# Half of the ktile pairs of the second MLP products with 7 block products in place of 8

## The chip, the cores and the metric

One core of a Trainium2 chip runs the whole program. The metric is the device time of one execution in microseconds; three runs of the kernel before gave 2282.13 to 2282.56 us, median 2282.18 us.

## The reference, cut to what matters

Two decoder layers work on x of 256 tokens by 2048 features in float32. Each layer has an attention part and an MLP, and each of the four sub-layers adds its normalised output to the stream:

```python
def sq_relu_mlp(h, w1, w2):
    return jnp.square(jax.nn.relu(h @ w1)) @ w2
...
h = h + rms_norm(sq_relu_mlp(rms_norm(h, g_pre), w1, w2), g_post)
```

w1 is 2048 x 8192 and w2 is 8192 x 2048. The change concerns the second product of each MLP, hidden (256 x 8192) times w2.

## The kernel before, in words

Every large product is made of two-part operands: `split` (lines 238 to 246) writes a float32 operand as a high part in float32r (ScalarE, line 242, or 245 where a gain is multiplied in) and the rest as a low part (VectorE, line 243 or 246). A product of x and w is then three matmuls: high·high, high·low, low·high. The weights come as raw tiles of two ktiles (a ktile is 128 rows) by 1024 columns, 1 MB, by SyncE's queue (line 310, three buffers). `weights` splits each ktile into one `whi` and one `wlo` tile of 128 x 1024, five buffers of each (`NW`). So ScalarE and VectorE prepare weights while TensorE multiplies, and five ktiles are the farthest that they can be ahead.

`mlp` (line 620) goes over four blocks b of 2048 hidden features. In each, `ff1` computes hidden = relu(u·w1)², two calls of `job_T` of 1024 features (lines 405 and 409 are its matmuls of 512 and of 256 columns). The evacuation of a PSUM bank there is a ScalarE copy of 256 columns (L398), a VectorE addition (L399), and for every two banks relu and square on ScalarE (L628, L629) and a split into the tile `hT` (L242, L243). Then two calls of `job` (line 324, its matmul is line 361) multiply the 16 ktiles of the block by w2, for columns 0 to 1023 and 1024 to 2047: per ktile 2 token tiles x 2 column chunks x 3 = 12 matmuls of 128 x 512. The four sums of a `job` are evacuated into the tiles `m`, which stay in SBUF over all blocks: a ScalarE copy in block 0 (L670), a VectorE addition later (L672). After the last block `PostNorm` squares, scales (GpSimd, L589) and adds to the stream h.

The large SBUF tiles (8 KB a partition) share one pool, `A`, of 11 buffers (`NA`): in the MLP 4 for the input `uT`, 4 for `hT`, 2 for `m`, 1 for the gain. The stream h has a place of its own. The six scratch tiles `s2` serve the evacuations. PSUM has 8 banks: 4 `mm`, 2 `sb`, 2 `tb`. Small pieces of other work are queued in `bt` and let in between products by a credit of time (`tick`).

The order of each engine's instructions is fixed at build time by the scheduler of the kernel's framework, which takes instructions as they become ready and, among ready ones, the earliest in the program. An engine runs its own list strictly in that order.

## Time and profile before

| | |
|---|---|
| median of three runs | 2282.18 us |
| the profiled execution, its own time | 2280.53 us |
| its span in the trace | 2278.6 us |
| TensorE (PE) matmuls | 11949, busy 99% of the span |
| VectorE (DVE) busy | 1346.2 us, 59% |
| ScalarE (ACT) busy | 1250.0 us, 55% |
| GpSimd (POOL) busy | 51.9 us, 2%; it issues no DMA |
| DMA | 418.58 MB, 184 GB/s over the span |
| granted TensorE clock | 0.998 of full speed, 2.4 GHz |

The profiled execution's own time holds 1.9 us that lie outside its span. A busy matmul time is not time on the path: matmuls overlap in the array, so the distance between starts counts. Idle time of an engine that isn't the bottleneck costs nothing by itself.

### The profile page before, as it was taken

How to read it: one execution, taken by the hardware profiler on the slowest of the kernel's cores; microseconds unless marked ns; L12 is line 12 of the kernel's file. 1: busy time of each engine (PE TensorE's matmuls, PEld its weight loads, DVE VectorE, ACT ScalarE, POOL GpSimd, SP SyncE). 2: the span in 40 equal slices, each digit the busy share in tenths (PEclk: the TensorE clock that was granted, in tenths of full speed). 3: DMA queues.
4: the chain of work that ended last, by engine and by line, in shares of the span. 5: the costliest groups of instructions: out<-in, count | busy, mean ns of one | idle time of the engine just before them, and what ended most of it. 6: DMA issues, size and time to landing. Idle time of an engine off the chain costs nothing.

```text
span 2278.6 us, 30208 instructions
## 1 busy us (share of the span) xinstructions
PE 2255.6 (99%) x11949; PEld 1937.5 (85%) x11949; DVE 1346.2 (59%) x2059; ACT 1250.0 (55%) x1940; POOL 51.9 (2%) x44
## 2 busy tenths in 40 slices
PE   9999999999999999999999999999999999999997
PEld 9889887888888888887888888887888888888886
DVE  5877547544654554566565677847554554554555
ACT  5766547544644544555556666657554554554553
POOL 0000010000000000011000000001000000000002
PEclk9999999999999999999999999999999999999999
DMA  7844455565465555554554554555565555555553
GB/s 249 247 148 139 140 174 166 198 208 186 168 220 185 185 203 185 185 198 160 188 193 149 184 174 159 178 174 163 192 212 188 188 198 189 186 198 190 185 202 112
DMA packets 131177, 418.58 MB, mean 184 GB/s; under 512 B 6870, under 2 KB 7644, under 8 KB 130524
## 3 DMA queue, kind: packets, MB, share of 16 engines
q1 hardware_dynamic: 131036, 416.66, 54.3%
q8 instruction: 93, 1.52, 0.3%
q14 instruction: 48, 0.39, 0.1%
HBM read 414.54 MB, written 2.10 MB: 183 GB/s over the span
## 4 chain that ended last, share of the span: by engine, by line
PE 90%; issue 5%; DVE 2%; POOL 1%; ACT 1%; DMA 0%; DVEq 0%; POOLq 0%; SPq 0%; ACTq 0%
PE mm L361 27%; PE mm L405 19%; PE mm L409 10%; PE sb L361 6%; PE tb L361 6%; PE tb L405 4%; PE sb L405 4%; PE sb L409 2%; PE tb L409 2%; PE mm L435 2%; PE sb L539 2%; PE mm L443 2%; PE tb L283 1%; DVE h L603 1%; POOL m L589 1%
## 5 line engine op out<-in xcount | busy, mean ns | idle before, releaser
L246 DVE SCALAR_TENSOR_TENSOR wlo<-raw,gT,whi 128x512 fp32r<-128x512 f32 (+4 forms) x621 | 606.6, 1010 | 433.5 <-PE tb L409 208.2
L245 ACT ACTIVATE whi<-raw,gT 128x512 fp32r<-128x512 f32 (+4 forms) x621 | 551.2, 928 | 452.3 <-PE tb L405 238.0
L243 DVE TENSOR_TENSOR wlo<-raw,whi 128x1024 fp32r<-128x1024 f32 x304 | 376.6, 1245 | 356.8 <-ACT whi L242 356.8
L242 ACT ACTIVATE whi<-raw 128x1024 fp32r<-128x1024 f32 x304 | 320.7, 1061 | 384.5 <-PE mm L361 212.3
L405 PE MATMUL mm<-uT,whi 128*128 128x512 f32 x1952 | 503.5, 394 | 0.3 <-ACT z L845 0.3
L405 PEld LDWEIGHTS mm<-uT,whi 128*128 128x128 f32 x1952 | 346.9, 189 | 58.4 <-DVE s L399 0.7
L409 PEld LDWEIGHTS mm<-uT,wlo 128*128 128x128 f32 x1952 | 271.2, 190 | 22.3
L409 PE MATMUL mm<-uT,wlo 128*128 128x256 f32 x1952 | 280.3, 283 | 0.0
L361 PE MATMUL mm<-whi,hT 128*128 128x512 f32 x1024 | 280.3, 389 | 0.0
L361 PEld LDWEIGHTS mm<-whi,hT 128*128 128x128 f32 x1024 | 192.3, 188 | 39.7
L361 PE MATMUL mm<-whi,uT 128*128 128x512 f32 (+1 forms) x640 | 197.0, 398 | 0.0
L361 PE MATMUL mm<-wlo,hT 128*128 128x512 f32 x512 | 162.9, 389 | 0.0
L361 PE MATMUL tb<-whi,hT 128*128 128x512 f32 x512 | 160.6, 390 | 0.0
L361 PE MATMUL sb<-whi,hT 128*128 128x512 f32 x512 | 160.3, 389 | 0.0
L361 PEld LDWEIGHTS mm<-whi,uT 128*128 128x128 f32 x640 | 116.0, 189 | 19.9 <-ACT uT L242 0.2
L405 PE MATMUL tb<-uT,whi 128*128 128x512 f32 x448 | 122.8, 390 | 0.0
L405 PE MATMUL sb<-uT,whi 128*128 128x512 f32 x448 | 122.4, 390 | 0.0
L361 PEld LDWEIGHTS sb<-whi,hT 128*128 128x128 f32 x512 | 96.1, 188 | 20.0
L361 PEld LDWEIGHTS tb<-whi,hT 128*128 128x128 f32 x512 | 96.0, 188 | 19.8
L361 PEld LDWEIGHTS mm<-wlo,hT 128*128 128x128 f32 x512 | 96.2, 188 | 19.6
L361 PE MATMUL mm<-wlo,uT 128*128 128x512 f32 x320 | 104.9, 385 | 0.3 <-DVE wlo L246 0.3
L405 PEld LDWEIGHTS sb<-uT,whi 128*128 128x128 f32 x448 | 82.1, 188 | 15.3
(269 smaller groups left out, 2516.9 us busy)
## 6 DMA issues: line engine op xcount, KB each, us to landing
raw<-in_l_w_ff_dram SPq DMA_DIRECT2D x256, 1024.0 KB, 5.0
raw<-in_l_w_in_dram SPq DMA_DIRECT2D x87, 1024.0 KB, 5.1
raw<-in_l_w_out_dram SPq DMA_DIRECT2D x24, 1024.0 KB, 5.0
raw<-in_l_w_in_dram SPq DMA_DIRECT2D x8, 832.0 KB, 4.7
raw<-in_l_w_in_dram SPq DMA_DIRECT2D x8, 536.0 KB, 4.2
raw<-in_l_mla_w_uq_dram SPq DMA_DIRECT2D x4, 768.0 KB, 4.5
h<-in_x_dram SPq DMA_DIRECT2D x8, 256.0 KB, 5.8
raw<-in_l_mla_w_ukv_dram SPq DMA_DIRECT2D x2, 1024.0 KB, 5.0
```

The source lines that it names most:

```text
L242: nc.scalar.activation(hi, src, AF.Copy)
L243: eng.tensor_tensor(lo, src, hi.bitcast(F), ALU.subtract)
L245: nc.scalar.activation(hi, src, AF.Copy, scale=scale)
L246: nc.vector.scalar_tensor_tensor(lo, src, scale, hi.bitcast(F), ALU.mult, ALU.subtract)
L283: nc.tensor.transpose(pv[:, i, :], src[:, i * P:(i + 1) * P], ident)
L361: nc.tensor.matmul(ps[t, c][:, 0:w], xs, ws[:, offs[c]:offs[c] + w], start=(k == 0 and p == 0), stop=(k == nk - 1 and p == 2))
L405: nc.tensor.matmul(ps[b], wt[0][:, fs], mov.both(k), start=(k == 0), stop=False, skip_group_check=True)
L409: nc.tensor.matmul(ps[b][:, 0:SEQ], wt[1][:, fs], mov.at(k)[0], start=False, stop=(k == nk - 1), skip_group_check=True)
L435: nc.tensor.matmul(ps[b][:, f * SEQ:(f + 1) * SEQ], ws[:, fs], xs, start=(k == 0 and p == 0 and f == 0), stop=(k == nk - 1 and p == 2 and ...
L443: nc.tensor.matmul(ps[b][:, at:at + w], xs[:, tsl(t)], part(ws), start=(k == 0 and p == 0 and i == 0), stop=(k == nk - 1 and p == 2 and i ...
L539: nc.tensor.matmul(ps[:, parts[t]], q[:, tsl(t)], k[:, 0:(t + 1) * P], start=(i == 0), stop=(i == len(terms) - 1))
L589: eng.tensor_tensor(self.m[t][:, s], self.m[t][:, s], self.g[:, s], ALU.mult)
```

## The change

Ktiles are taken in pairs (2k, 2k+1), so a pair with 1024 columns is a 2 x 2 by 2 x 2 block product: token tiles by ktiles, and ktiles by column chunks. Of the 8 pairs of a block, pairs 4 to 7 use 7 block products of sums (`SEVEN`) instead of 8; pairs 0 to 3 keep 8. The two kinds alternate (`order`: 0, 4, 1, 5, 2, 6, 3, 7). `job_7` does this for both column halves c of every block, except columns 1024 to 2047 of the last block, which still use `job`.

- Activations: `Sevens.put` makes four sums of the hidden blocks of a pair (one subtraction of 256 columns, two of 128) and splits them (512 columns) at the end of `ff1`.
- Weights: `seven_weights` makes three sums of 1024, 512 and 512 elements a partition in float32, and splits the two raw halves, the two sums t1 and t3 (1024) and t4 (512). t1 and t3 lie in a tile of pool `A` (`wboth`), as the raw sums do (`wsum`); the rest in the five `whi` and `wlo` buffers.
- Results: eight accumulators (four of `c`, and p1, p5, p6, p7) take all 8 PSUM banks. They are combined linearly, so over blocks 0 to 2 they are kept uncombined in DRAM: a ScalarE copy to `s2`, then a GpSimd DMA of 256 KB, a plain write in block 0 and an accumulating one after. In the last block `combine` loads them (SyncE's queue) and adds them up on VectorE beside `ff1`, and `into` adds the last block's banks.
- SBUF: `m` exists in the last block alone, h goes into two tiles of pool `A`, is written to DRAM by GpSimd's queue in block 0 and loaded again in the last block. `A` has 13 buffers.

The places where `h[:, t, ...]` becomes `h[t][:, ...]` are left out.

```diff
@@ -35,7 +35,7 @@
 STEP_US = 1.28
-NA, NW = 11, 5
+NA, NW = 13, 5
 WARM = 8
...
@@ -84,6 +84,7 @@
     wraw = ctx.enter_context(tc.tile_pool(name="wraw", bufs=3))
+    dram = ctx.enter_context(tc.tile_pool(name="dram", bufs=1, space=bass.MemoryType.DRAM))
     whl = ctx.enter_context(tc.tile_pool(name="whl", bufs=NW))
...
@@ -170,7 +174,7 @@
     gr0, gr1, per = grow[0:16, 0, :], grow[0:54, 1, :], grow[0:64, 2, :]
-    h = cst.tile([P, T, D], F, name="h")
+    h = [A([P, D], F, f"h{t}") for t in range(T)]
     w2kv = cst.tile([P, 2, P], F, name="w2kv")
...
@@ -466,6 +470,103 @@
+    class Sevens:
+        def __init__(self, stat, pairs):
+            self.stat, self.pairs = stat, pairs
+            self.tiles = [A([P, 2, 2, 512], R, "sums") for _ in range((len(pairs) + 1) // 2)]
+        def put(self, pair, y):
+            f = s2()
+            base = y[:, 0:P]
+            two = bass.AP(tensor=base.tensor, offset=base.offset, ap=[base.ap[0], [3 * P, 2], [1, P]])
+            nc.vector.tensor_tensor(
+                f[:, 0:2 * P].rearrange("p (i q) -> p i q", i=2),
+                y[:, P:2 * P].unsqueeze(1).to_broadcast([P, 2, P]), two, ALU.subtract)
+            nc.vector.tensor_tensor(f[:, 2 * P:3 * P], y[:, 0:P], f[:, P:2 * P], ALU.subtract)
+            nc.vector.tensor_tensor(f[:, 3 * P:4 * P], y[:, 2 * P:3 * P], f[:, 2 * P:3 * P], ALU.subtract)
+            i = self.pairs.index(pair)
+            split(self.tiles[i // 2][:, i % 2, 0, :], self.tiles[i // 2][:, i % 2, 1, :], f)
+        def at(self, pair, which):
+            if which in SUMS:
+                i, q = self.pairs.index(pair), tsl(SUMS.index(which))
+                v = self.tiles[i // 2][:, i % 2, :, q]
+                return v[:, 0, :], v[:, 1, :]
+            t, k = which
+            return self.stat.at(2 * pair + k, t)
+    SUMS = ("s3", "s1", "s2", "s4")
+    def seven_weights(W, k0, c0, order, sevens):
+        for pair in order:
+            raw = wraw.tile([P, 2, 1024], F, name="raw")
+            r0 = (k0 + 2 * pair) * P
+            nc.sync.dma_start(raw, W[r0:r0 + 2 * P, c0:c0 + 1024].rearrange("(k p) c -> p k c", p=P))
+            parts = {}
+            def part(src, names, hi, lo):
+                split(hi, lo, src)
+                for i, name in enumerate(names):
+                    parts[name] = hi[:, i * 512:i * 512 + 512], lo[:, i * 512:i * 512 + 512]
+            if pair not in sevens.pairs:
+                for k in range(2):
+                    part(raw[:, k, :], [(k, 0), (k, 1)], W4("whi"), W4("wlo"))
+                yield parts
+                continue
+            sums = A([P, 4, 512], F, "wsum")
+            flat = raw.rearrange("p k c -> p (k c)")
+            b11, b12, b21, b22 = (flat[:, i * 512:i * 512 + 512] for i in range(4))
+            outer = bass.AP(tensor=b11.tensor, offset=b11.offset, ap=[b11.ap[0], [1536, 2], [1, 512]])
+            nc.vector.tensor_tensor(sums[:, 0:2, :], outer, b12.unsqueeze(1).to_broadcast([P, 2, 512]), ALU.add)
+            nc.vector.tensor_tensor(b12, sums[:, 0, :], b22, ALU.add)
+            nc.vector.tensor_tensor(sums[:, 2, :], b12, b21, ALU.add)
+            part(raw[:, 1, :], [(1, 0), (1, 1)], W4("whi"), W4("wlo"))
+            part(raw[:, 0, :], [(0, 0), "t2"], W4("whi"), W4("wlo"))
+            both = A([P, 2, 1024], R, "wboth")
+            part(sums[:, 0:2, :].rearrange("p i c -> p (i c)"), ["t1", "t3"], both[:, 0, :], both[:, 1, :])
+            part(sums[:, 2, :], ["t4"], W4("whi")[:, 0:512], W4("wlo")[:, 0:512])
+            yield parts
+    SEVEN = (("c11", (0, 1), (1, 0)), ("c12", "s4", (1, 1)), ("p1", (0, 0), (0, 0)), ("p6", "s2", "t2"),
+             ("p5", "s1", "t1"), ("p7", "s3", "t3"), ("c21", (1, 1), "t4"))
+    LAST_SEVEN = tuple(SEVEN[i] for i in (0, 1, 6, 2, 4, 3, 5))
+    def job_7(sevens, W, k0, c0, order, evac):
+        gen = seven_weights(W, k0, c0, order, sevens)
+        ps = {}
+        def seq_of(pair):
+            if pair in sevens.pairs:
+                return LAST_SEVEN if pair == order[-1] else SEVEN
+            return tuple((f"c{t + 1}{n + 1}", (t, k), (k, n)) for k in range(2) for t in range(T) for n in range(2))
+        last = {}
+        for j, pair in enumerate(order):
+            for i, (b, _, _) in enumerate(seq_of(pair)):
+                last[b] = (j, i)
+        for j, pair in enumerate(order):
+            parts = next(gen)
+            seq = seq_of(pair)
+            for i, (b, which, form) in enumerate(seq):
+                xh, xl = sevens.at(pair, which)
+                wh, wl = parts[form]
+                first = b not in ps
+                if first:
+                    ps[b] = (mm_bank if b[0] == "c" else s_bank if b in ("p1", "p6") else t_bank)()
+                for p, (xs, ws) in enumerate(((xh, wh), (xh, wl), (xl, wh))):
+                    nc.tensor.matmul(ps[b], xs, ws, start=first and p == 0, stop=last[b] == (j, i) and p == 2,
+                                     skip_group_check=True)
+                bt.tick(3 * 512 / 2400)
+                if last[b] == (j, i):
+                    evac(b, ps[b])
     def chunks512(c0, n=1024):
...
@@ -571,8 +672,8 @@
-        def __init__(self, gname, eps=None):
-            self.m = [A([P, D], F, "m") for _ in range(T)]
+        def __init__(self, gname, eps=None, m=None):
+            self.m = m or [A([P, D], F, "m") for _ in range(T)]
             self.parts = [sml.tile([P, 8], F, name="pparts", tag="pparts", bufs=4) for _ in range(T)]
...
@@ -622,21 +723,29 @@
         nk = FBLK // P
-        pn = None
+        order = [p for i in range(nk // 4) for p in (i, nk // 4 + i)]
+        BANKS = ("c11", "c12", "c21", "c22", "p1", "p5", "p6", "p7")
+        acc = [{b: dram.tile([P, 512], F, name=f"acc{c}{b}", tag=f"{gname}{c}{b}") for b in BANKS} for c in range(2)]
+        kept = [dram.tile([P, D], F, name=f"kept{t}", tag=f"{gname}kept{t}") for t in range(T)]
...
-        def ff1(b, hT):
+        def ff1(b, hT, sevens):
             def evac(t, c, ps):
...
                 def f(i, y):
-                    hT.put(i0 + 2 * i, 2, None, relu2(y, y).rearrange("p (f q) -> p f q", f=2))
+                    k = i0 + 2 * i
+                    relu2(y, y)
+                    hT.put(k, 2, None, y.rearrange("p (f q) -> p f q", f=2))
+                    if k // 2 in sevens.pairs:
+                        sevens.put(k // 2, y)
                 return f
...
@@ -649,33 +758,108 @@
-        eps = []
+        def ff2(b, sevens, c, evac):
+            job_7(sevens, w2, b * nk, c * 1024, order, evac)
+        def to_acc(b, c):
+            def f(name, ps):
+                y = s2()
+                nc.scalar.activation(y, ps, AF.Copy)
+                if b == 0:
+                    nc.gpsimd.dma_start(acc[c][name], y)
+                else:
+                    nc.gpsimd.dma_start(acc[c][name], y, accum_op=ALU.add)
+            return f
+        def out_of(m, c, t, n):
+            return m[t][:, c * 1024 + n * 512:c * 1024 + n * 512 + 512]
+        def combine(m, c):
+            pt = A([P, 4, 512], F, "pt")
+            p = {}
+            for i, name in enumerate(BANKS[4:]):
+                p[name] = pt[:, i, :]
+                nc.sync.dma_start(p[name], acc[c][name])
+            for t in range(T):
+                for n in range(2):
+                    nc.sync.dma_start(out_of(m, c, t, n), acc[c][f"c{t + 1}{n + 1}"])
+            for _ in range(4):
+                yield
+            o = lambda t, n: out_of(m, c, t, n)
+            add = nc.vector.tensor_tensor
+            for dst, x, y, op in (
+                    (p["p6"], p["p6"], p["p1"], ALU.subtract), (o(0, 0), o(0, 0), p["p1"], ALU.add),
+                    (p["p5"], p["p5"], p["p6"], ALU.add), (o(0, 1), o(0, 1), p["p5"], ALU.add),
+                    (o(1, 1), o(1, 1), p["p5"], ALU.add), (o(1, 1), o(1, 1), p["p7"], ALU.add),
+                    (p["p6"], p["p6"], p["p7"], ALU.add), (o(1, 0), o(1, 0), p["p6"], ALU.subtract)):
+                add(dst, x, y, op)
+                yield
+        def into(pn, c, m):
+            got = {}
+            def f(name, ps):
+                got[name] = y = s2()
+                nc.scalar.activation(y, ps, AF.Copy)
+                o = lambda t, n: out_of(m, c, t, n)
+                def add(dst, y, op=ALU.add):
+                    nc.vector.tensor_tensor(dst, dst, y, op)
+                if name[0] == "c":
+                    add(o(int(name[1]) - 1, int(name[2]) - 1), y)
+                elif name == "p1":
+                    add(o(0, 0), y)
+                    pn.chunk_done(0, 2 * c)
+                elif name == "p6":
+                    add(y, got["p1"], ALU.subtract)
+                    add(got["p5"], y)
+                    add(o(0, 1), got["p5"])
+                    pn.chunk_done(0, 2 * c + 1)
+                    add(o(1, 1), got["p5"])
+                elif name == "p7":
+                    add(o(1, 1), y)
+                    pn.chunk_done(1, 2 * c + 1)
+                    add(got["p6"], y)
+                    add(o(1, 0), got["p6"], ALU.subtract)
+                    pn.chunk_done(1, 2 * c)
+            return f
+        eps, m = [], None
         for b in range(nb):
             hT = Split("hT", nk)
-            ff1(b, hT)
+            sevens = Sevens(hT, tuple(range(nk // 4, nk // 2)))
+            end = b == nb - 1
+            if end:
+                m = [A([P, D], F, "m") for _ in range(T)]
+                for c in range(2):
+                    bt.add(combine(m, c))
+            ff1(b, hT, sevens)
             if b == 0:
...
                     eps.append(e)
-                pn = PostNorm(gname, eps)
-            end = b == nb - 1
-            def evac(base):
-                def f(t, c, ps):
-                    cc = base + c
-                    m = pn.m[t][:, cc * 512:(cc + 1) * 512]
-                    if b == 0:
-                        nc.scalar.activation(m, ps, AF.Copy)
-                    else:
-                        nc.vector.tensor_tensor(m, ps, m, ALU.add)
-                    if end:
-                        pn.chunk_done(t, cc)
-                return f
-            job(hT, w2, b * nk, nk, chunks512(0), evac(0))
-            job(hT, w2, b * nk, nk, chunks512(1024), evac(2), last=4 if end else 1, bank=all_banks(4),
-                after=(lambda t: pn.finish(t, then)) if end else None)
+                    nc.gpsimd.dma_start(kept[t], h[t])
+                    h[t] = None
+            if not end:
+                for c in range(2):
+                    ff2(b, sevens, c, to_acc(b, c))
+                continue
+            bt.flush()
+            pn = PostNorm(gname, eps, m)
+            ff2(b, sevens, 0, into(pn, 0, m))
+            for t in range(T):
+                h[t] = A([P, D], F, f"h{t}")
+                nc.sync.dma_start(h[t], kept[t])
+            def evac(t, c, ps):
+                o = m[t][:, 1024 + c * 512:1536 + c * 512]
+                nc.vector.tensor_tensor(o, ps, o, ALU.add)
+                pn.chunk_done(t, 2 + c)
+            job(hT, w2, b * nk, nk, chunks512(1024), evac, last=4, after=lambda t: pn.finish(t, then))
```

## Rows read from the trace of the kernel before

**Rows 1.** The page: busy time, share of the span and instructions by engine.

```profile
span 2278.6 us, 30208 instructions
...
PE 2255.6 (99%) x11949; PEld 1937.5 (85%) x11949; DVE 1346.2 (59%) x2059; ACT 1250.0 (55%) x1940; POOL 51.9 (2%) x44
```

**Rows 2.** Windows, layer 0: second products, blocks 0 and 1; `ff1` of block 1 between.

```profile
core 0: us, PE busy (x) PEld busy (x) DVE busy (x) ACT busy (x) POOL busy (x), PEclk, DMA share, GB/s
...
443.40:530.60 87.20, 87.20 (x387) 72.24 (x386) 44.28 (x40) 43.48 (x52) 0.00 (x0) 1.00 0.60 207
530.60:619.70 89.10, 89.10 (x514) 78.47 (x513) 45.69 (x48) 46.84 (x63) 0.00 (x0) 1.00 0.56 189
619.70:706.80 87.10, 87.10 (x386) 72.14 (x385) 47.31 (x46) 39.78 (x45) 0.00 (x0) 1.00 0.56 194
```

**Rows 3.** The chain of waits, in order of time: start, us, what.

```profile
443.59 43.55 PE mm L361 x192
...
1115.91 3.65 PE mm L405 x16
1119.57 1.91 PE mm L409 x16
```

**Rows 4.** Groups by form, whole span: busy us, mean ns | idle before, releaser.

```profile
L243 DVE TENSOR_TENSOR wlo<-raw,whi 128x1024 fp32r<-128x1024 f32 x304 | 376.6, 1245 | 356.8 <-ACT whi L242 356.8
...
L242 ACT ACTIVATE whi<-raw 128x1024 fp32r<-128x1024 f32 x304 | 320.7, 1061 | 384.5 <-PE mm L361 212.3 <-PE tb L361 134.3 <-PE tb L405 27.7
...
L399 DVE TENSOR_TENSOR s<-mm,s 128x256 f32<-128x256 f32 x122 | 47.9, 417 | 8.8 <-ACT s L398 8.3
...
L243 DVE TENSOR_TENSOR hT<-s,hT 128x512 fp32r<-128x512 f32 x60 | 41.3, 688 | 17.2 <-ACT hT L242 15.9
...
L242 ACT ACTIVATE hT<-s 128x512 fp32r<-128x512 f32 x60 | 38.0, 633 | 0.0
...
L672 DVE TENSOR_TENSOR m<-mm,m 128x512 f32<-128x512 f32 x24 | 15.4, 684 | 6.5 <-PE mm L361 6.5
...
L1102 DVE TENSOR_SCALAR o_acc<-o_acc,ca 128x128 f32<-128x128 f32 x32 | 8.1, 278 | 0.0
```

**Rows 5.** Timeline of DVE and of ACT in steady second products; last bracket: idle before.

```profile
477.38 1.23 DVE L243 TENSOR_TENSOR wlo<-raw,whi 128x1024 fp32r<-128x1024 f32 x1 [1.50 <-ACT whi L242]
...
476.29 1.06 ACT L242 ACTIVATE whi<-raw 128x1024 fp32r<-128x1024 f32 x1 [1.66 <-PE mm L361]
```

**Rows 6.** Windows of 15 us about the eight starts of second products, first and last.

```profile
438.70:453.70 15.00, 15.00 (x75) 12.60 (x74) 11.84 (x18) 13.60 (x25) 0.00 (x0) 1.00 0.63 214
...
2175.20:2190.20 15.00, 15.00 (x75) 12.61 (x74) 11.84 (x19) 13.45 (x25) 0.00 (x0) 1.00 0.46 148
```

**Rows 7.** Timeline of PE's first second product and of DVE's low parts before it.

```profile
443.43 0.40 PE L361 MATMUL mm<-whi,hT 128*128 128x512 f32 x1
...
433.64 1.22 DVE L243 TENSOR_TENSOR wlo<-raw,whi 128x1024 fp32r<-128x1024 f32 x1
438.00 2.36 DVE L243 TENSOR_TENSOR wlo<-raw,whi 128x1024 fp32r<-128x1024 f32 x2 [3.15 <-ACT whi L242]
...
447.45 1.22 DVE L243 TENSOR_TENSOR wlo<-raw,whi 128x1024 fp32r<-128x1024 f32 x1 [1.04 <-ACT whi L242]
```

**Rows 8.** DMA issues: out<-in, engine, count, KB each, median us to landing.

```profile
raw<-in_l_w_ff_dram SPq DMA_DIRECT2D x256, 1024.0 KB, 5.0
...
gpost<-in_l_norm_ffn_post_dram SPq DMA_DIRECT2D x2, 1024.0 KB, 9.1
out_dram<-h SPq DMA_DIRECT2D x8, 256.0 KB, 2.6
```

**Rows 9.** Waits of SyncE's queue: us in total, times, longest us.

```profile
SPq L310 <- DVE wlo L243: 692.2, 140, 9.0
```

**Rows 10.** Timeline of ACT at the evacuation of a `job`, block 0.

```profile
485.42 2.35 ACT L670 ACTIVATE m<-mm 128x512 f32<-128x512 f32 x4
```

**Rows 11.** Timeline near the end: GpSimd's gains and DVE's low parts beside them.

```profile
2225.28 5.56 POOL L589 TENSOR_TENSOR m<-m,gpost 128x512 f32<-128x512 f32 x3 [0.86 <-ACT junk L236]
...
2227.70 1.99 DVE L243 TENSOR_TENSOR wlo<-raw,whi 128x1024 fp32r<-128x1024 f32 x1 [1.44 <-ACT whi L242]
2230.02 1.91 DVE L243 TENSOR_TENSOR wlo<-raw,whi 128x1024 fp32r<-128x1024 f32 x1 [0.33 <-ACT whi L242]
2232.74 1.23 DVE L243 TENSOR_TENSOR wlo<-raw,whi 128x1024 fp32r<-128x1024 f32 x1 [0.81 <-ACT whi L242]
```

More of the change, by code (lines that the diff above doesn't have):

```diff
@@ L96, in A, with W4 @@
         return big.tile(shape, dt, name=name, tag="A")
+    def W4(name):
+        return whl.tile([P, 1024], R, name=name)
     def mm_bank():
@@ L184, in load_x @@
         for t in range(T):
[L185 removed]
+            nc.sync.dma_start(h[t][:, c * 512:(c + 1) * 512], x[:, t, c * 512:(c + 1) * 512])
     def load_rot():
@@ L286, in h_to @@
     def h_to(dst, t, c):
-        dst.put(4 * c, 4, t, transposed(h[:, t, c * 512:(c + 1) * 512], 4, s_bank() if c % 2 else None))
+        dst.put(4 * c, 4, t, transposed(h[t][:, c * 512:(c + 1) * 512], 4, s_bank() if c % 2 else None))
     def h_sum(t):
@@ L291, in h_sum @@
         for c in range(4):
-            square_sum(parts[:, c:c + 1], h[:, t, c * 512:(c + 1) * 512], D)
+            square_sum(parts[:, c:c + 1], h[t][:, c * 512:(c + 1) * 512], D)
         return sum_eps(parts, 4)
@@ L315, in weights @@
                     if at == 0:
-                        his = whl.tile([P, 1024], R, name="whi")
-                        los = whl.tile([P, 1024], R, name="wlo")
+                        his = W4("whi")
+                        los = W4("wlo")
                     hi, lo = his[:, at:], los[:, at:]
@@ L600, in finish @@
                     nc.scalar.activation(self.m[t][:, s], self.m[t][:, s], AF.Copy, scale=r)
-                    nc.gpsimd.tensor_tensor(h[:, t, s], self.m[t][:, s], h[:, t, s], ALU.add)
+                    nc.gpsimd.tensor_tensor(h[t][:, s], self.m[t][:, s], h[t][:, s], ALU.add)
                 else:
-                    nc.vector.scalar_tensor_tensor(h[:, t, s], self.m[t][:, s], r, h[:, t, s], ALU.mult, ALU.add)
+                    nc.vector.scalar_tensor_tensor(h[t][:, s], self.m[t][:, s], r, h[t][:, s], ALU.mult, ALU.add)
                 if c < 3:
@@ L695, in start @@
                 for t in range(T):
-                    uT.put(i, 2, t, transposed(h[:, t, i * P:(i + 2) * P], 2, s_bank() if t else None))
+                    uT.put(i, 2, t, transposed(h[t][:, i * P:(i + 2) * P], 2, s_bank() if t else None))
         if k in AHEAD:
@@ L1182, in then_out @@
         s = slice(c * 512, (c + 1) * 512)
-        nc.sync.dma_start(ov[:, t, s], h[:, t, s])
+        nc.sync.dma_start(ov[:, t, s], h[t][:, s])
     mlp(uT, a["l1_w_ff1"], a["l1_w_ff2"], gT, 32, h_sum, "l1_norm_ffn_post", then_out)
```

1 line of the change is left out of this document (removed).

## The prediction

> **What bounds the kernel now.** The page comes first [rows 1]: PE is busy 99% of the span, DVE 59%, ACT 55%. A busy share alone proves little, since matmuls overlap, so the windows over the MLP come next [rows 2]: a block's second products take 87.1 to 87.2 us and its first products 89.1 us, with PE busy in all of it and DVE and ACT in about half. The chain of waits then gives the distance between matmuls [rows 3]: a `job` is one unbroken piece of 43.55 us for 192 matmuls of 512 columns, 226.8 ns each, and two of them (87.10) fill the window of the second products. The first products show the same: 3.65 + 1.91 = 5.56 us for two ktiles, 16 ktiles twice make 89.0 us. So PE runs in the MLPs without a gap, at the full clock (1.00 in every window), and a matmul that is left out is worth its 226.8 ns, as long as the other engines keep up.
>
> The timeline shows why they now do [rows 5]: ACT waits 1.66 us for PE to give a `whi` buffer back, DVE then 1.50 us for ACT, at each ktile. Both are ahead and idle.
>
> **What is removed.** A pair of ktiles by 1024 columns takes 24 matmuls, 5.44 us; a pair with 7 block products takes 21, 4.76 us. Such pairs: 4 per column half, 7 column halves per layer (the last half of the last block keeps `job`), 2 layers: 56. That is 56 x 3 = 168 matmuls, **38.1 us**. Nothing is added on PE: sums are made on DVE. The Trainium skill gives 215.7 ns between starts for 512 columns (TensorE: Matmul & The Clock Gate, section "Wait — 56ns, not 53.3ns?"); 168 of those would be an estimated 36.2 us, while the chain here has 226.8 and decides.
>
> **DVE and ACT in steady second products.** By the rows for 1024, 512, 256 and 128 elements [rows 4], an ordinary pair costs DVE 2 x 1.245 = 2.49 us. A 7-product pair costs sums of 1024, 512, 512 (1.245 + 2 x 0.684) and low parts of 3 x 1024 and 512 (3 x 1.245 + 0.688): 7.04 us. Two pairs cost DVE 9.53 us beside 5.44 + 4.76 = 10.21 us of PE, 93%. ACT has 5 x 1.061 + 0.633 = 5.94 us. So PE still is the longest, with 0.7 us to spare in each two pairs. Buffers allow it: five `whi`/`wlo` tiles hold one ordinary pair (2) and one 7-product pair (3), the fourth part lies in `A`, and the sums need no such tile, so they can go before a buffer is free. Cost taken: 0. Lost cover is a case below.
>
> **Start of the second products.** This is where cover is thinnest. In the 15 us about each of the eight starts, DVE is busy 11.84 us and ACT 13.45 to 13.60 [rows 6], because the evacuation of the first products meets the first weight splits. The change adds on DVE four times `put` (0.417 for 256, 2 x 0.278 for 128, 0.688 for the low part: 1.66 us) = 6.6 us, and 7.04 − 2.49 = 4.55 us for the first 7-product pair. Of that the sums and one low part (2.61 + 1.245 = 3.86 us) can go earlier, in the idle time of `ff1`, where only the `A` pool is needed. So 11.84 + 6.6 + 4.55 − 3.86 = 19.1 us of work in 15.0: 4.1 us too much. Against it stands the lead that weights have: the first product starts at 443.43, so the fourth ktile is wanted 3 x 2.72 us later, at 451.6, and its low part (the fourth in the timeline) is done at 448.7 [rows 7]: 2.9 us. I take 4.1 − 2.9 = **1.2 us** for each of eight starts, 9.6 us. Bounds: 0, if the scheduler puts `put` of the later pairs behind the weights (pair 7 is used last), and 6.9 us, where ACT's excess (13.6 + 4 x 0.633 + 1.061 + 0.633 − 15 = 2.8) comes on top of the 4.1 and nothing of the lead is left: 0 to 55 us in all. I take the low third since DVE idles 3.2 us in these windows today.
>
> **Ends of the second products.** Eight banks are evacuated by ACT copies (2.35 us for four [rows 10]) in place of four, each into one of six `s2` tiles that stays taken until the GpSimd store has landed. No row shows a store from GpSimd or an accumulating one. Nearest is the plain store of 256 KB from SyncE's queue, 2.6 us to landing; the slowest large transfer of the MLP took 9.1 us [rows 8]. The seventh evacuation (p6) is due 6 products of 0.68 us = 4.1 us after the first (c22), and its tile is free at 0.59 + 2.6 = 3.2 us: no wait by the near row, 5.6 us by the far one. Where the other column half follows, p6's bank is wanted only some 7 us later (5.44 for the ordinary pair, then its place in the 7): covered. Where `ff1` follows (6 times) all 8 banks are wanted within 3.2 us. I take 0.5 us each, near the low end, **3 us**; bounds 0 and 34.
>
> **Last block.** `into` has 12 DVE additions for the first column half where 4 stood: 8 x 0.684 = 5.5 us more, ahead of the weights of the last `job`. Their lead is 2.9 us, and DVE idles 1.5 us a ktile there, so I take 1 us per layer, **2 us**; bounds 0 and 11. `combine` adds 16 x 0.684 = 11 us of DVE work per layer inside `ff1`, where DVE is half idle: 0. Its 16 loads and the two of h stand in SyncE's queue before weight loads. A store that lands late would hold the weights behind it; but that queue itself waits for DVE to free raw buffers, 692 us in 140 waits [rows 9], 4.9 us a wait. With a landing of 9.1 us in place of 5.0 the spare 4.9 us still covers it: 0; bounds 0 and 4 us per layer. h in DRAM costs DMA alone, in block 0 and the last: 0, and at most one 9.1 us landing per layer where `wboth` waits for h's tiles.
>
> **DMA.** Added are 96 stores of 0.26 MB, 64 of them reading the sum too, 32 loads, and h out and in: about 59 MB on 419, some 212 GB/s. The windows of second products already carried 207 [rows 2]: 0.
>
> **GpSimd beside DVE.** One row speaks against the change: while GpSimd's gains run, DVE's low part takes 1.99 and 1.91 us, 1.23 after them [rows 11]. If issuing a store did that, eight would cost DVE 8 x 0.76 = 6 us at the end of a column half. The Trainium skill (SBUF — State Buffer, "Who interferes with whom") says that a DVE instruction with two SBUF inputs contends with a GpSimd instruction that reads SBUF, and infers that descriptor writing, which needs the write side, isn't held up by tensor_tensor. Rows 11 agree with its first half; no run here shows a GpSimd DMA. By its second half the cost is 0, by the first half's measure 6 us at twelve ends. I take 0, and the rest is in the third rival.
>
> **The sum.** 38.1 − 9.6 − 3 − 2 = 23.5 us gained. The profiled execution took 2280.53 us (span 2278.6, 1.9 outside); it becomes 2257.0. The median of the three runs stands 1.65 us above it: **2258.7 us**.
>
> **Rivals.**
> 1. *All covered.* The starts cost nothing, as they cost nothing today [rows 2, 3]. Then 38.1 us go: 2244 us. For: PE had no gap at any start. Against: 19.1 us of DVE work in 15. Chance 0.13, for 2243 to 2250.
> 2. *DVE becomes the bound of the second products* (slower). Today every low part waits for its high part [rows 5], and DVE's list is strictly in order. If DVE stands idle for one high part of 1.06 us in each two pairs, the period is 10.59 us, the 38.1 become 56 x (10.89 − 10.59) = 17 us, and with 14.6 of costs nothing is left: 2280 us. If twice, 11.65 us: over 10.89, the two ordinary pairs of today, from which the change loses by itself: 56 x 0.76 = 43 us lost, 2325 us without and 2339 with the 14.6 us. For: 93% leaves 0.7 us. Against: the sums need no high part and can fill the waits. Chance 0.12 for the slower form.
> 3. *Stores hold up the evacuations or DVE.* With a landing of 9.1 us six ends cost 5.6 us each, and 6 us of DVE at the six other ends comes out at perhaps half: 34 + 18 = 52 in place of the 3: 2308 us. For: rows 11, and no row for such stores. Against: the plain store's 2.6 us. Chance 0.07. Half of it, or one wait of rival 2, gives 2274 to 2290, around no change: chance 0.13.
> 4. *The change does less than it says.* The 168 matmuls are counted in the code, and no cover hides work on PE, so I give this nothing of its own.
>
> **How the numbers follow.** The forecast with its bounds near (2250 to 2274 us) has 0.55, rival 1 0.13, the middle 0.13, rivals 2 and 3 in their slower forms 0.19. A measurement of this kernel tells about 0.2%, 4.6 us, from no change. Faster than 2277.6: 0.55 + 0.13 + 0.04 of the middle = 0.72. Within: 0.08. Slower than 2286.7: 0.01 + 0.19 = 0.20. The range takes in the forecast, rival 1 and the middle: 2243 to 2290 us, 0.81.
>
> **What the profile after would show.** Right: 11781 matmuls at about 227 ns; DVE busy near 1346 + 56 x 4.55 + 32 x 1.66 + 11 = 1665 us, 74%; a steady two pairs in 10.2 us with PE unbroken; gaps of one to two us at the eight starts, ended by DVE's low parts or ACT's high parts. Wrong: two pairs in over 10.9 us with PE waiting for DVE throughout (rival 2); ACT waiting for a GpSimd queue at the ends (rival 3); SyncE's loads late behind `combine`.

## The result and the profile after

Four runs of the changed kernel gave 2338.29 to 2340.86 us, median 2339.77, against 2281.69 to 2282.56 us, median 2282.15, for the kernel before. The ratio is **1.0252, 95% interval 1.0234 to 1.0270**: 57.6 us slower, where 23.5 us faster was forecast and 2290 us was the upper end of the range.

The page of the kernel after, its first part (it answers to [rows 1]):

```profile
span 2337.8 us, 31006 instructions
...
PE 2256.1 (97%) x11781; PEld 1921.1 (82%) x11781; DVE 1624.5 (69%) x2483; ACT 1405.9 (60%) x2180; POOL 128.7 (6%) x144
```

The 168 matmuls are gone (11949 to 11781), yet PE is busy as long as before. With fewer matmuls that means that some ran slower, and PE is idle for 2337.8 − 2256.1 = 81.7 us of the span, where it was 23.0 before. The windows of layer 0's stages say where (columns as in [rows 2], to which they answer): second products of block 0, `ff1` of block 1, second products of block 1, `ff1` of block 2.

```profile
444.85:534.50 89.65, 84.75 (x362) 68.98 (x361) 78.52 (x95) 60.80 (x80) 6.96 (x13) 0.96 0.60 206
534.50:623.60 89.10, 89.10 (x514) 78.44 (x513) 48.19 (x50) 48.23 (x62) 1.62 (x4) 1.00 0.62 218
623.60:715.10 91.50, 85.47 (x363) 68.17 (x361) 78.29 (x95) 60.70 (x80) 10.11 (x13) 0.96 0.63 196
715.10:809.20 94.10, 91.19 (x514) 79.73 (x513) 48.22 (x50) 48.23 (x62) 4.02 (x5) 0.98 0.67 212
```

The second products have 24 matmuls fewer per block and take 2.5 to 4.4 us more, with PE idle for 5 to 6 us and a granted clock of 0.96. `ff1` of block 1 is unchanged; that of block 2, whose code for PE is the same as before, takes 5 us more. The first start, cut into four windows, shows the loss of the second products:

```profile
446.00:451.70 5.70, 5.70 (x26) 4.50 (x24) 4.29 (x12) 5.09 (x11) 0.00 (x0) 1.00 0.01 3
451.70:456.20 4.50, 0.14 (x1) 0.00 (x0) 4.47 (x11) 3.96 (x7) 0.00 (x0) 0.94 0.01 2
456.20:462.00 5.80, 5.26 (x12) 3.52 (x13) 5.80 (x9) 4.94 (x6) 0.00 (x0) 0.50 0.07 11
462.00:465.00 3.00, 3.00 (x14) 2.46 (x13) 3.00 (x4) 0.38 (x1) 0.00 (x0) 0.93 1.04 347
```

PE runs for a few us on the first, ordinary pair and two products of the next, stands for 4.4 us (one matmul in 4.5 us), and then has the lower of its two clocks, 1.2 GHz, for 5.8 us: 12 matmuls where 226.8 ns each would make 25. The waits name what it stood for, in us in total, times and the longest:

```profile
ACT wboth L246 <- DVE wsum L525: 84.0, 39, 4.8
...
PE tb L564 <- ACT wboth L246: 35.0, 8, 4.4
...
ACT s L767 <- DMA acc0c<-s: 17.9, 7, 4.7
ACT s L767 <- DMA acc1c<-s: 17.6, 8, 4.1
```

Eight times, once at each start, PE waits 4.4 us for ACT's high part of t1 and t3 (`wboth`), and ACT for the weight sums from DVE (`wsum`). DVE's timeline at the first start shows that it wasn't idle but occupied with other things:

```profile
452.47 0.74 DVE L403 TENSOR_TENSOR s<-tb,s 128x256 f32<-128x256 f32 x2
453.25 0.69 DVE L247 TENSOR_TENSOR sums<-s,sums 128x512 fp32r<-128x512 f32 x1
453.86 1.22 DVE L525 TENSOR_TENSOR wsum<-raw 128x1024 f32<-128x1024 f32 x1
```

PE's timeline has the end of that wait (in brackets, PE's idle time before it):

```profile
456.22 1.22 PE L564 MATMUL tb<-wboth,sums 128*128 128x512 f32 x2 [4.38 <-ACT wboth L246]
```

The first sum of the first 7-product pair runs at 453.86, after the low part of one of the activation sums (`sums`), although PE has come to the product with t1 4.38 us before 456.22, at 451.8. The second loss is in the other two lines of the waits: ACT stood 35.5 us for a scratch tile `s2` whose store (`acc0c`, `acc1c`) had not landed. The DMA issues give the reason (KB each, median us to landing, as in [rows 8]):

```profile
acc0c<-s POOLq DMA_DIRECT2D x24, 256.0 KB, 7.4
acc0p<-s POOLq DMA_DIRECT2D x24, 256.0 KB, 10.9
```

These medians mix the plain stores of block 0 with the accumulating ones of blocks 1 and 2. Apart, in layer 0, block 0 (plain, 444 to 530 us) and then block 1 (accumulating, 618 to 712 us):

```profile
acc0c<-s POOLq DMA_DIRECT2D x4, 256.0 KB, 5.1
acc0p<-s POOLq DMA_DIRECT2D x4, 256.0 KB, 7.9
...
acc0c<-s POOLq DMA_DIRECT2D x4, 256.0 KB, 8.5
acc0p<-s POOLq DMA_DIRECT2D x4, 256.0 KB, 11.0
```

Here is how long layer 0's stages take in every kernel of this study, from PE's first matmul of a stage to that of the next, in us:

| kernel | second products, blocks 0, 1, 2 | `ff1`, blocks 1, 2, 3 |
|---|---|---|
| before | 87.06, 87.06, 87.07 | 89.07, 89.07, 89.06 |
| after | 89.67, 91.51, 91.85 | 89.07, 94.06, 94.59 |
| e1_early_tiles | 81.85, 83.91, 84.49 | 89.28, 95.72, 99.82 |
| e2_own_f | 87.73, 90.98, 90.24 | 89.08, 91.67, 97.94 |
| e3_early_tiles_own_f | 81.67, 85.36, 84.66 | 89.07, 94.20, 97.74 |
| e4_plain_store | 89.51, 88.97, 90.31 | 89.09, 89.08, 89.12 |
| e5_p_banks_in_A | 83.29, 89.65, 91.07 | 89.08, 89.06, 100.23 |
| e6_paced_loads | 81.68, 85.09, 84.31 | 89.08, 92.91, 95.92 |
| e7_all | 82.01, 90.91, 89.87 | 89.08, 89.09, 95.37 |
| e8_paced_plain | 81.67, 81.67, 81.64 | 89.08, 90.13, 90.55 |
| e9_ordinary_pair_last | 83.39, 86.20, 84.21 | 90.27, 93.10, 94.17 |
| e10_eight_s2 | 81.87, 84.22, 84.21 | 89.09, 89.07, 96.08 |
| e11_seven_s2_own_f | 81.66, 84.68, 85.46 | 89.12, 89.08, 92.48 |

### The profile page after: what moved, and what is told of

Same layout as the page of the kernel before. It is cut to its first block, busy times and chain, and to the rows that moved or that the text cites. A ratio compares the mean times of both kernels' runs of the same rounds, so it can differ in the third digit from the quotient of the medians.

```text
span 2337.8 us, 31006 instructions
## 1 busy us (share of the span) xinstructions
PE 2256.1 (97%) x11781; PEld 1921.1 (82%) x11781; DVE 1624.5 (69%) x2483; ACT 1405.9 (60%) x2180; POOL 128.7 (6%) x144
## 5 line engine op out<-in xcount | busy, mean ns | idle before, releaser
L247 DVE TENSOR_TENSOR wlo<-raw,whi 128x1024 fp32r<-128x1024 f32 x304 | 374.3, 1245 | 139.1 <-ACT whi L246 134.2
L246 ACT ACTIVATE whi<-raw 128x1024 fp32r<-128x1024 f32 x304 | 313.2, 1055 | 147.7 <-PE mm L365 66.7
L564 PE MATMUL mm<-whi,hT 128*128 128x512 f32 x1120 | 359.9, 393 | 0.0
L564 PEld LDWEIGHTS mm<-whi,hT 128*128 128x128 f32 x1120 | 212.9, 190 | 44.7
L564 PE MATMUL mm<-wlo,hT 128*128 128x512 f32 x560 | 219.5, 392 | 0.6 <-DVE wlo L247 0.6
L564 PE MATMUL tb<-wboth,sums 128*128 128x512 f32 x336 | 100.9, 425 | 35.0 <-ACT wboth L246 35.0
L564 PEld LDWEIGHTS mm<-wlo,hT 128*128 128x128 f32 x560 | 105.6, 189 | 25.2 <-DVE wlo L247 3.6
L564 PEld LDWEIGHTS tb<-wboth,sums 128*128 128x128 f32 x336 | 66.9, 204 | 54.0 <-ACT wboth L246 38.4
L246 ACT ACTIVATE wboth<-wsum 128x1024 fp32r<-128x1024 f32 x56 | 59.5, 1062 | 85.8 <-DVE wsum L525 84.0
L409 PEld LDWEIGHTS tb<-uT,whi 128*128 128x128 f32 x448 | 81.4, 189 | 23.6 <-ACT s L767 7.6
```

The costliest lines, as they stand in the source:

```text
L246: nc.scalar.activation(hi, src, AF.Copy)
L247: eng.tensor_tensor(lo, src, hi.bitcast(F), ALU.subtract)
L409: nc.tensor.matmul(ps[b], wt[0][:, fs], mov.both(k), start=(k == 0), stop=False, skip_group_check=True)
L564: nc.tensor.matmul(ps[b], xs, ws, start=first and p == 0, stop=last[b] == (j, i) and p == 2, skip_group_check=True)
```

## The experiments

All are edits of the changed kernel. The kernel before, beside them, had a median of 2281.46 to 2281.91 us, to which the ratios refer.

### The starts: why the weight sums come late

The tiles of pool `A` are asked for in the program in the order `hT`, `sums`, and then, with the weights of the second products, `wsum` and `wboth`. One theory was that the order of asking is the order of handing out: the last `sums` tile is first written only when pair 6 is evacuated, and until then no `wsum` can have a buffer. A rival was the scratch `f` of `put`, which takes an `s2` tile that the next evacuations want. The third was plain work: DVE can't do more in that time, as the prediction's 19.1 us in 15 had it.

**e1_early_tiles** writes one column of each of these tiles as soon as it exists.

```diff
             sevens = Sevens(hT, tuple(range(nk // 4, nk // 2)))
+            for part in hT.parts + sevens.tiles:
+                nc.gpsimd.memset(part[:, 0, 0, 0:1].bitcast(F), 0.0)
```

> Same work as the changed kernel; the hT and sums tiles of a block get a one-column GpSimd memset when they are made, so that pool A hands them out before wsum. Theory (order of handing out): wsum cannot be handed out before the last sums tile, whose first write is ScalarE's of pair 6, so the weight sums of the first 7-product pair stand behind nearly all evacuations in DVE's list; with the tiles taken early the eight starts lose their 4.4 us wait and the stretch at the lower clock behind it (together some 7.5 us each, 60 us): 2275 to 2290 us. Rival (DVE has too much to do at the starts, whatever its order): the work is the same, so at most 15 us go: 2325 us or more.

Measured: 2287.4 us (2284.0 to 2291.95), ratio 1.0027 [1.0017, 1.0037]. Of the 57.6 us lost, 52.4 are back.

**e2_own_f** gives `f` a buffer of its own and leaves the rest.

```diff
-            f = s2()
+            f = scr.tile([P, 512], F, name="f", tag="f", bufs=1)
```

> The scratch f of the hidden sums gets one buffer of its own instead of one of the six s2. Theory (order of handing out): the ScalarE copies of the next bank pair no longer stand behind f, so the evacuation chain of four bank pairs gets some 3 us shorter, but wsum still stands behind the sums tile: each of eight starts gains 1 to 3 us, 2316 to 2332 us. Rival (too much work on DVE): no change, 2340 us.

Measured: 2328.51 us (2325.55 to 2332.3), ratio 1.0207 [1.0192, 1.0222]: 11.3 us back.

**e3_early_tiles_own_f** has both edits.

> Both edits. Theory (order of handing out): all eight starts without a wait of PE over 0.5 us, ends as in the changed kernel: 2270 to 2285 us. Rival (too much work on DVE): 2320 us or more, with PE waiting 2 us or more at each start.

Measured: 2286.62 us (2283.09 to 2288.89), ratio 1.0019 [1.001, 1.0029]. That is 1.6 us above the range that was expected, far from the rival's 2320 us, and PE's waits for `wboth` are gone. Together the two edits give 53.2 us, no more than e1 alone within the intervals; they act on the same wait. The timeline of DVE in e1 at the first start:

```profile
437.21 1.22 DVE L525 TENSOR_TENSOR wsum<-raw 128x1024 f32<-128x1024 f32 x1
...
443.38 1.22 DVE L247 TENSOR_TENSOR wboth<-wsum,wboth 128x1024 fp32r<-128x1024 f32 x1
...
449.67 1.22 DVE L525 TENSOR_TENSOR wsum<-raw 128x1024 f32<-128x1024 f32 x1
```

The sums of the first 7-product pair begin at 437.21, where the changed kernel began them at 453.86, and at 443.38 the low part of t1 and t3 is made; at 449.67 DVE is at the second pair. The windows of e3, block 0's second products and then the first three of the four stretches above:

```profile
444.00:526.00 82.00, 82.00 (x364) 67.80 (x363) 73.56 (x90) 57.83 (x77) 7.76 (x20) 1.00 0.65 226
446.00:451.70 5.70, 5.70 (x27) 4.64 (x26) 5.70 (x12) 5.70 (x10) 0.00 (x0) 1.00 0.00 1
451.70:456.20 4.50, 4.50 (x21) 3.70 (x21) 4.50 (x8) 3.74 (x6) 0.00 (x0) 1.00 0.80 253
456.20:462.00 5.80, 5.80 (x28) 4.79 (x27) 5.80 (x10) 4.78 (x6) 0.00 (x0) 1.00 0.56 182
```

PE no longer stands and the clock stays at 1.00. DVE and ACT are busy in every us from 446 to 451.7: the same work fits, only its order differs. So it is the order of the tiles that held the sums back, not the amount of work; the third theory falls. With PE unbroken, the block takes 81.67 us.

### The stores

**e4_plain_store** writes the blocks of the results without adding them up.

```diff
-                    nc.gpsimd.dma_start(acc[c][name], y, accum_op=ALU.add)
+                    nc.gpsimd.dma_start(acc[c][name], y)
```

> The GpSimd stores of blocks 1 and 2 are plain writes, so blocks are not added up (that part of the computation is left out). Theory (accumulating stores hold the s2 buffers too long): ff1 of blocks 2 and 3 goes from 94.1 to 95.0 us back to the 89.1 us of block 1, which follows plain stores: some 21 us less, 2319 us. Rival (the ends wait for ScalarE or DVE themselves): ff1 of blocks 2 and 3 stays over 93 us and the time at 2340 us.

Measured, in one run, so without an interval: 2311.67 us, 28 us less than the changed kernel, where 21 were expected. `ff1` of blocks 2 and 3 is back at 89.1 us. The second products of blocks 1 and 2 gain 2.5 and 1.5 us, which was not expected, and keep the rest of their loss: the starts are as they were, and PE still waits 35.0 us for `wboth`.

**e5_p_banks_in_A** is e3, and the four p banks are evacuated into one tile of pool `A` in place of four `s2`.

```diff
+            hold = []
             def f(name, ps):
-                y = s2()
+                if name[0] == "p":
+                    if not hold:
+                        hold.append(A([P, 4, 512], F, "po"))
+                    y = hold[0][:, BANKS.index(name) - 4, :]
+                else:
+                    y = s2()
```

> E3's edits, and the banks p1, p5, p6, p7 are evacuated into one tile of pool A instead of four s2 tiles, so that no evacuation waits for an earlier store. Theory (accumulating stores hold s2 too long): the waits of ScalarE for acc stores (38 us in all in e3) and PE's gaps at the starts of ff1 of block 2 (3 to 4 us with the lower clock behind them, two layers) go, and the 2 to 3 us over 81.7 us in the second products of blocks 1 and 2; ff1 of block 3 stays long by its weight loads: 2264 to 2275 us. Rival (the DMA engines are full there, so the weights are late whatever the buffers): 2283 us or more.

Measured: 2307.08 us (2303.78 to 2309.88), ratio 1.011 [1.0096, 1.0124], a miss. The waits of e5 show why:

```profile
DVE wsum L525 <- DMA acc0p<-po: 55.4, 6, 11.1
...
PE mm L564 <- DVE wlo L247: 28.6, 6, 6.7
```

The evacuations no longer wait (`ff1` of block 2: 89.06), but the tile `po` stays taken until its stores land, `A` has no other to give to `wsum`, and DVE waits up to 11.1 us for it at a change of column half. The wait was moved to a costlier place.

**e6_paced_loads** is e3, and the 16 loads of `combine` are spread over `ff1`: each waits, through a one-column copy by GpSimd, for the low part of the weights made last, and gives way twice.

```diff
+    recent = [None]
+    def paced_load(dst, src):
+        nc.gpsimd.tensor_copy(dst[:, 0:1], recent[0][:, 0:1].bitcast(F))
+        nc.sync.dma_start(dst, src)
...
+                    recent[0] = lo
...
+            for _ in range(4 if c == 0 else 0):
+                yield
...
-                nc.sync.dma_start(p[name], acc[c][name])
+                paced_load(p[name], acc[c][name])
+                yield
+                yield
...
-                    nc.sync.dma_start(out_of(m, c, t, n), acc[c][f"c{t + 1}{n + 1}"])
+                    paced_load(out_of(m, c, t, n), acc[c][f"c{t + 1}{n + 1}"])
+                    yield
+                    yield
```

> E3's edits, and the 16 loads of combine are spread over ff1 of the last block, each tied to a weight split by a one-column GpSimd copy. Theory (sixteen loads of 0.26 MB at once beside the stores of column half 1 keep the weights away): ff1 of block 3 goes from 98 to 100 us to 91 to 94 us, two layers: 2272 to 2278 us. Rival (block 3 loses by the store waits at its start alone): ff1 of block 3 stays over 96 us, 2283 us or more.

Measured: 2277.45 us (2275.78 to 2279.95), ratio 0.9981 [0.9972, 0.999]: 9.2 us less than e3. In e3 the stores of block 2 and the loads of `combine` met at the start of `ff1` of block 3; its windows and, behind them, a line of ACT's timeline:

```profile
885.00:890.00 5.00, 5.00 (x31) 4.43 (x30) 1.89 (x2) 2.50 (x3) 0.54 (x1) 1.00 1.11 263
...
895.00:900.00 5.00, 3.25 (x22) 2.81 (x21) 2.50 (x4) 0.18 (x1) 0.00 (x0) 1.00 1.04 398
900.00:905.00 5.00, 3.63 (x9) 2.57 (x10) 3.56 (x4) 2.00 (x2) 0.00 (x0) 0.66 1.05 398
```

```profile
899.82 2.19 ACT L249 ACTIVATE whi<-raw,gT 128x1024 fp32r<-128x1024 f32 x2 [12.32 <-DMA raw<-in_l_w_ff_dram]
```

The DMA engines are full (share over 1.0), at 263 GB/s while the stores are under way and at 398 after. ACT waits 12.3 us for a raw tile, and PE, out of weights, stands and then gets a clock of 0.66. The same windows in e6:

```profile
885.00:890.00 5.00, 3.93 (x16) 3.75 (x17) 2.48 (x2) 4.58 (x5) 2.04 (x3) 0.50 1.11 226
...
895.00:900.00 5.00, 5.00 (x31) 4.39 (x30) 0.28 (x1) 1.91 (x2) 0.00 (x0) 1.00 1.05 401
900.00:905.00 5.00, 5.00 (x31) 4.47 (x30) 4.10 (x5) 2.31 (x2) 1.71 (x2) 1.00 0.37 121
```

In the later two PE is unbroken. Its gap is now at 882 to 890, where the evacuations wait for the stores. So `ff1` of block 3 gains only 1.8 us in layer 0, to 95.92, above the 91 to 94 that were expected; in layer 1 it gains 6.0 us, to 93.93.

**e7_all** has the edits of e5 and e6.

> All four edits. Theory (the 38.1 us of matmuls are real, and what the changed kernel lost is waits for buffers and loads): ff1 near 89 us in every block and the second products near 82 us: 2246 to 2258 us, faster than both kernels. Rival (DVE at 93% in the second products, or DMA, takes the rest): 2270 us or more.

Measured: 2296.77 us (2294.55 to 2298.14), ratio 1.0064 [1.0051, 1.0078], a miss for the reason that e5 showed.

**e8_paced_plain** is e6 with the plain stores of e4: what is left when neither the starts nor the accumulation cost anything.

> E6's kernel with plain stores in blocks 1 and 2, so blocks are not added up (that part of the computation is left out). Theory (what e6 lacks of the 38 us is held back by accumulating stores alone): ff1 at 89 to 90 us and second products at 82 us in all blocks but the last, 2250 to 2260 us. Rival (the rest is DVE at 93% in the second products of blocks 1 and 2): those stay at 84 to 85 us, and 2265 us or more.

Measured: 2251.4 us (2251.13 to 2252.12), ratio 0.9867 [0.9852, 0.9882], 26.0 us less than e6. The second products of block 1 in e8, in one window:

```profile
616.00:697.60 81.60, 81.60 (x362) 67.44 (x361) 73.55 (x89) 57.32 (x77) 7.54 (x20) 1.00 0.63 223
```

And its stores, plain, from GpSimd's queue:

```profile
acc0c<-s POOLq DMA_DIRECT2D x24, 256.0 KB, 5.4
acc0p<-s POOLq DMA_DIRECT2D x24, 256.0 KB, 7.5
```

### The order of the pairs, and more scratch tiles

**e9_ordinary_pair_last** is e6 with the last two pairs exchanged, so that the p banks end an ordinary pair earlier than the c banks. In the last block the squares for the norm are then taken before the c banks of that block are added, which changes that part of the computation and not its amount.

```diff
+        order = order[:-2] + [order[-1], order[-2]]
...
-                return LAST_SEVEN if pair == order[-1] else SEVEN
+                return LAST_SEVEN if pair == max(sevens.pairs) else SEVEN
```

> E6's kernel with the last two pairs of each column half exchanged, so that an ordinary pair ends it and p1, p5, p6, p7 are final 5.4 us earlier than the c banks; two 7-product pairs then stand next to each other. Theory (evacuations wait since eight stores of 7 to 11 us are asked for within 5 us): starts of ff1 gain 2 to 4 us in blocks 2 and 3, 2262 to 2272 us. Rival (two neighbouring 7-product pairs ask 14.1 us of DVE beside 9.5 us of PE, with no buffers for six parts): each column half loses 2 us or more, 2290 us or more.

Measured: 2298.28 us (2295.46 to 2298.76), ratio 1.0068 [1.0056, 1.0081], a miss: 20.8 us more than e6. The waits of e9:

```profile
ACT s L775 <- DMA acc0p<-s: 19.3, 7, 3.5
ACT s L775 <- DMA acc1p<-s: 15.5, 10, 3.0
```

The c banks now are the late ones and wait for the tiles of the p stores, 34.8 us in all; the wait follows whichever banks come last. With that, the starts of `ff1` gain little (93.10 and 94.17, for 92.91 and 95.92 in e6). Most of the loss, however, is in the second products of the last block, which take 93.46 us for 86.33 in e6, and as much more in layer 1. The waits in that stretch of layer 0 (977 to 1071 us):

```profile
ACT whi L246 <- DMA raw<-in_l_w_ff_dram: 7.2, 1, 7.2
...
PE mm L372 <- DVE wlo L247: 4.1, 1, 4.1
```

ACT waits 7.2 us for a raw tile there (3.1 in e6), and PE stands once for 4.1 us. Why the tile is late in this order was not tried. The time is in the rival's range, but not for the rival's reason: it had each column half lose 2 us or more, and the second products of blocks 0 to 2, two halves each, lose 1.7, 1.1 and nothing in layer 0 and 3.8, 1.5 and 0.4 in layer 1.

**e10_eight_s2** is e1 with the paced loads and eight `s2` (the attention's `p` has two buffers in place of three to make room).

```diff
-    scr = ctx.enter_context(tc.tile_pool(name="scr", bufs=6))
+    scr = ctx.enter_context(tc.tile_pool(name="scr", bufs=8))
...
-        p = att.tile([P, 3 * P], F, name="p", bufs=3)
+        p = att.tile([P, 3 * P], F, name="p", bufs=2)
```

> E1's early tiles and E6's paced loads, with eight s2 tiles in place of six (the attention's p tile has two buffers in place of three for room) and f from s2 again. Theory (a column half's eight evacuations wait because six s2 tiles come back only when accumulating stores land): ScalarE's waits for acc stores nearly vanish, ff1 of blocks 2 and 3 falls to 89 to 91 us, 2255 to 2266 us. Rival (f taken from s2 again lengthens the starts, and the waits move to the next use of s2 or to the weights' loads): 2275 us or more.

Measured: 2271.92 us (2270.48 to 2276.55), ratio 0.9961 [0.9948, 0.9975], above what it was expected to give: `ff1` of block 2 is at 89.07 us, but that of block 3 stays at 96.08.

**e11_seven_s2_own_f** is e6 with seven `s2` beside the one of `f`, and `p` as in e10.

```diff
-    scr = ctx.enter_context(tc.tile_pool(name="scr", bufs=6))
+    scr = ctx.enter_context(tc.tile_pool(name="scr", bufs=7))
...
-        p = att.tile([P, 3 * P], F, name="p", bufs=3)
+        p = att.tile([P, 3 * P], F, name="p", bufs=2)
```

> E6's kernel with seven s2 tiles in place of six (and two p buffers in the attention for room). Theory (s2 come back late): one evacuation per end waits instead of two, half of what e10 gains over e6: 2265 to 2272 us. Rival (the attention pays for its lost buffer, or the waits move): 2277 us or more.

Measured: 2269.38 us (2266.18 to 2270.35), **ratio 0.9943 [0.993, 0.9955]**: the shortest of those that leave nothing out, 0.6% under the kernel before. It gains 8.1 us on e6; half of e10's gain of 5.5 us was expected. The waits of ACT for the stores in e11, against 35.5 us after:

```profile
ACT s L774 <- DMA acc0c<-s: 6.2, 6, 1.8
...
ACT s L774 <- DMA acc1c<-s: 2.5, 2, 1.3
```

What is left of them lies elsewhere. Block 1's second products in e11 have a gap that e8 has not:

```profile
616.20:701.00 84.80, 82.76 (x363) 67.31 (x362) 73.67 (x90) 57.57 (x77) 10.72 (x20) 1.00 0.67 213
```

The waits in that window, in us in total, times and the longest:

```profile
DVE wsum L532 <- DMA raw<-in_l_w_ff_dram: 6.9, 3, 3.6
```

The same wait in e8 (616 to 698 us):

```profile
DVE wsum L532 <- DMA raw<-in_l_w_ff_dram: 2.6, 2, 2.2
```

And, among e11's DMA issues, the stores of the p banks:

```profile
acc0p<-s POOLq DMA_DIRECT2D x24, 256.0 KB, 13.5
```

DVE waits 6.9 us for raw weights, where it waited 2.6 in e8. e11 differs from e8 in the kind of store, one scratch tile and one buffer of the attention. e6 differs from e8 in the kind of store alone, and its second products of block 1 take 85.09 us for 81.67, so it is the accumulation that costs them time. The pages of e6 and then of e8 show that it also loads the DMA engines (GpSimd's queue: packets, MB, share of the 16 engines' time):

```profile
q0 software_dynamic: 12352, 29.37, 5.7%
...
q0 software_dynamic: 8256, 29.37, 3.4%
```

For the same bytes the queue has 4096 packets more and takes 5.7% of the engines' time in place of 3.4%. That the weights come late for this reason fits, but it is inferred: no run changes the engines' load and leaves the rest.

## Why the prediction was wrong, point by point

**The account.** From 2339.8 us, the order of the tiles gives 53.2 (e3), the spreading of `combine`'s loads 9.2 (e6) and the accumulation 26.0 (e8): 2251.4. The sizes hold in this order, since the obstacles change each other (see the last block below). What the change could give by its matmuls alone is 2282.15 − 38.1 = 2244.0. Of the 7.4 us between, `ff1` of blocks 2 and 3 has 1.06 + 1.49 us in layer 0 of e8 and 0.3 in layer 1 (89.09 and 89.33). The first second products begin 1.7 us later than before (445.15 for 443.43); where the rest lies is open. Rival 1 (2244 us, 2243 to 2250) is thus nearly what the change comes to, but in a kernel that leaves the accumulation out; of those with the whole result none came under 2266 us.

**What is removed: right.** 168 matmuls went, and where PE is not held up each is worth its 226.8 ns: a block's second products have 360 matmuls left, 360 x 0.2268 = 81.6, and e3 and e8 show 81.67.

**DVE and ACT in steady second products: right.** Rival 2 said that 93% of DVE would not do. In e8 all three blocks take 81.64 to 81.67 us with DVE busy 73.55 of 81.60 (90%). Rival 2's dearer form gave 2339 us, which is what was measured, but by a mechanism that isn't there: the loss is one gap at each start and not a longer period. Over the whole span DVE came to 1624.5 us where 1665 was expected.

**Start of the second products: the step that failed.** It said that the sums and one low part "can go earlier, in the idle time of `ff1`, where only the `A` pool is needed", and took 1.2 us for each start, with 0 to 6.9 as bounds. The pool was the obstacle itself. It had buffers enough (e1 has the same 13), but it gave none to `wsum` before the last `sums` tile, asked for earlier and first written only at the evacuation of pair 6, had its own. So those 3.86 us of DVE work stood behind nearly the whole evacuation, DVE reached them at 453.86, and PE waited 4.4 us. The second error was to price a stop at its length. After 4.4 us at rest PE had the lower clock, and 12 matmuls ran in the time of 25, some 3 us more. Against e3 block 0 took 89.67 − 81.67 = 8.0 us too much, above the 6.9 us bound, blocks 1 and 2 took 6.2 and 7.2. All eight second products are some 61 us longer than in e3's trace, where 9.6 were taken and 55 was the bound; `ff1` of blocks 2 and 3 is some 10 us longer in e3, so 53.2 us show in the time. The idle time of DVE in the windows of today [rows 6] was real, but not open to this work. The prediction counted work and buffers; it did not read in which order the pool hands them out.

**Ends of the second products: the wrong end of the bounds.** The seventh evacuation does wait for its `s2` tile, as the step worked out, but the near row (2.6 us [rows 8]) was taken for the store, and the far one (9.1) was nearer: 8.5 us for the c banks and 11.0 for p in block 1. The 3 us became 26.0, inside the bounds of 0 and 34. By the traces of e6 and e8, whose executions lie 28.6 us apart, `ff1` of blocks 2 and 3 have 2.8 + 5.4 us of it in layer 0 and 6.2 + 4.6 in layer 1. The second products of blocks 1 and 2, which the step did not have, have 3.4 + 2.7 and 2.3 + 2.1. The Trainium skill (DMA: Bandwidth & Descriptors, section "Anatomy of one DMA — SWDGE (gpsimd) path") fits a DMA from GpSimd with some 2.0 us and the bytes over 436 GB/s, an estimated 2.6 us for 256 KB. Four plain stores of e4 that were the first of a column half came near it (888 to 891.3 us):

```profile
acc1c<-s POOLq DMA_DIRECT2D x4, 256.0 KB, 2.9
```

As a rule the stores here, eight at a time and among the weight loads, took longer: medians of 5.4 to 7.9 us for the plain ones of e8, 8.5 and 11.0 accumulating in block 1. So the measurement decides against that figure for this place.

**Last block: right in this kernel, not in the mended one.** `combine`'s loads were taken at 0 with a bound of 4 us per layer, on the ground that the weights have 4.9 us to spare. In the changed kernel `ff1` of block 3 takes 94.59 us (94.72 in layer 1), within 0.6 us of block 2 with its 94.06 (94.95), and in e4, with the same loads and plain stores, it takes 89.12 (89.67). It is after the starts were mended that the loads cost something: in e3 `ff1` of block 3 takes 97.74 us, with 12.3 us of waiting for one raw tile beside the stores of block 2, and spreading the loads gave 9.2 us over two layers, a little over the bound of 8. The 2 us for `into` don't show: the last block's second products take 86.32 us in e3 and 89.76 before, 3.4 us less, where its 12 matmuls are worth 2.7.

**GpSimd beside DVE: right.** The low parts took 1245 ns on average before [rows 4] and 1245 after:

```profile
L247 DVE TENSOR_TENSOR wlo<-raw,whi 128x1024 fp32r<-128x1024 f32 x304 | 374.3, 1245 | 139.1 <-ACT whi L246 134.2 <-PE mm L564 4.9
```

So issuing the stores cost DVE nothing that shows, as the second half of the Trainium skill's rule had it (SBUF — State Buffer, "Who interferes with whom"), and that half of rival 3 falls. Its other half, stores with a landing of 9.1 us that hold the evacuations, is what happened, at about the price that it gave (34 us, measured 26, of which some 19 at the ends by the traces).

**The chances.** Slower had 0.20, from rivals 2 and 3. The largest loss was in neither; the range could only have held it if the starts had been given a case of their own with what a stop does to the clock.

## What to carry to other kernels

Work can move into idle time only if the buffers it needs can be given out that early: read in which order tiles of one pool are asked for and when the earlier ones are first written, not only how many there are. A stop of TensorE is to be priced with the slower matmuls behind it, which the windows show by granted clock and matmul count. A store that accumulates in DRAM is to be measured beside the loads that it will run with before its buffers are counted. What an obstacle costs depends on the others: the loads of `combine` cost 9.2 us only once the starts were mended.
